# The short branch's output projection by seven half-block products in two duals, with its operands' sums behind the last input dual

## The chip, the cores and the metric

The kernel is written for one Trainium2 core and runs on one. Its time is device microseconds of one execution; the kernel before has a median of 1498.0 us over three runs (1496.49 to 1498.34). The engines are TensorE (PE, with its weight loads as PEld), VectorE (DVE), ScalarE (ACT), GpSimd (POOL) and SyncE (SP), which here issues most of the loads. Each engine, and each queue of DMA issues, works through its own list in order; they meet through semaphores.

## The reference

One block of a streaming encoder on 1024 positions (T) of 1024 channels (D), in float32:

```
h    = rms_norm(x, g) * (1 + sc1) + sh1              # sh1, sc1, g1, ... = silu(c) @ w_ada + b_ada
b_s, c_s, v_s, v_c, gl_c, gates = split(h @ w_in)
y_a  = (b_s * causal_dwconv3(c_s * v_s)) @ w_short_out
u    = causal_dwconv31(v_c * sigmoid(gl_c)) + bias
y_b  = silu(layer_norm(u)) @ w_conf_out
g_a, g_b = split(sigmoid(gates))
x    = x + g1 * ((g_a * y_a + g_b * y_b) @ w_o)
x    = x + g2 * swiglu_ffn(rms_norm(x) * (1 + sc2) + sh2)
out  = rms_norm(x, g_final)
```

## The kernel before, in words

**Products.** A float32 product is made of three matmuls: an operand is split into a rounded high part and the rest (`split`: a cast on ACT, a subtraction on DVE), a weight likewise into `wh` and `wl` (`split_w`: the cast on ACT, `wl = raw - wh` on DVE or POOL), and `mm3` issues high by high, low by high and high by low (L286, L287, L289). Matmuls are 128x128 by 128x512; T is handled in halves of 512.

**Duals.** The input projection runs, after a lead, in 12 duals (`win_dual`). A dual treats two output column blocks together and multiplies 2 by 2 blocks with seven half-block products in place of eight, in the order `PRODUCTS` ("1265734"). Each of the seven takes 24 matmuls and its own weight tile, partly a sum of blocks of the matrix (`dual_units`: "s1" is a21+a22, and so on; in the duals POOL makes the sums and the low parts). Its results are sums of the products, made as they come out: `c11`, `c22`, `c12` and `c21` do that on DVE and ACT. `PAIRS` says which columns a dual makes: gates ("g"), products of the short branch ("p", "q"), or the conv branch's input ("u"). The short branch leaves `q`, eight tiles of 128 x 1024, stored to DRAM by `q_store`.

**Beside the duals** DVE runs the eight long convs, tap by tap (L674), paced over `CONV_DUALS` duals by `issue_after`; POOL adds each conv to a total (`add_conv`) for the layer norm.

**Then ya**, the product with `w_short`: eight column blocks (`col_block`), each with one weight tile of 1024 columns and 48 matmuls, giving both halves; DVE multiplies each by the gate `ga`, loaded by POOL's queue, into `ma` (L765). In between come mean and variance (`ln_mean`, `ln_square`, `ln_rstd`) and eight `modulation`s (a product of the conditioning vector with a column block of `w_ada`, one long DVE instruction each). `q_load` brings q back from DRAM in the last dual and splits all of it there.

**Then yb** (`row_blocks` over `w_conf`, with `act_b` one block ahead and 16 modulations, in `next_b`), where `gb` is multiplied in and `join` adds `ma`; **then** `mix` with `w_o`, and the feed-forward part, again in duals.

**What sets the order.** The code is written in the order in which a tile scheduler takes it; tiles come from pools whose buffers wait for their last reader (raw weights have 3 + 2 buffers, `wh` and `wl` 3 each, gate tiles 6, PSUM 6 + 2 banks). Weights are fetched `AHEAD` (2) units before use, from `plan`. Where the code says `issue_after`, an instruction is held behind another.

Of the kernel before, what the change touches and what calls it, by code (L numbers as in the profile page):

```python
# [37 lines left out]
ALU = mybir.AluOpType  # L38
# [44 lines left out]

CONV_DUALS = 11.2
AT_READS = {"7": 4.5, "3": 5.5, "4": 6.5}
# [25 lines left out]
def block_kernel(ctx: ExitStack, tc: tile.TileContext, x0, xT, c, vecs, ada, w_first, w_plain, w_duals,  # L111
# [101 lines left out]

    def dual_units(mats, n, early=False, eng=nc.vector):

        a = {}

        def get(*blocks):
            for b in blocks:
                a[b] = load(mats[("11", "12", "21", "22").index(b)], n)  # L220

        def unit(m):
            if early:
                get(*{"1": ("11",), "2": ("12",), "6": ("21", "22", "11"), "3": ("12",), "4": ("22",)}.get(m, ()))
            elif m == "1":
                get("11", "12", "21", "22")
            if m in "12":
                return split_w(a["1" + m], n, (), eng)
            if m == "6":
                a["s1"] = a["22"] if early else raw_tile(n)  # L230
                eng.tensor_tensor(a["s1"], a["21"], a["22"], ALU.add)  # L231
# [4 lines left out]
            return split_w(a[{"6": "11", "5": "s1", "7": "21", "3": "12", "4": "22"}[m]], n, (), eng)  # L236

        return {m: (lambda m=m: unit(m)) for m in PRODUCTS}
# [314 lines left out]

    qT = [[None, None] for _ in range(KC)]

    def q_load(j):

        t = uc_tile("q", T)
        nc.sync.dma_start(t, q_dram[j])
        for h in range(2):  # L560
            qT[j][h] = split(t[:, halves[h]], hl_tile, f"q{j}{h}")

    def win_dual(d, pairs, x, y, z):
# [4 lines left out]
        def c11(p, e, kind, j, *more):  # L568
            if kind == "q":
                times(sc[j][:, halves[0]], y[p], sc[j][:, halves[0]])  # L570
                return
            if kind == "u":
                u.append(u_tile(j))
                e["b"] = [u[j][:, CK - 1 + h * H : CK - 1 + (h + 1) * H] for h in range(2)]
            elif kind == "p":
                e["t"] = uc_tile(f"p{j}", T + SK - 1)
                nc.vector.memset(e["t"][:, : SK - 1], 0.0)
                e["b"] = [e["t"][:, SK - 1 + h * H : SK - 1 + (h + 1) * H] for h in range(2)]
            else:
                e["t"] = [uc_tile("sig", T) for _ in range(2)]  # L580
                e["b"], e["c"] = ([t[:, s] for s in halves] for t in e["t"])
            nc.scalar.activation(e["b"][0], y[p], AF.Sigmoid if kind == "g" else AF.Copy)

        def c22(p, e, kind, j, *more):
            src = y[p] if kind == "q" else e["5"]
            add = nc.vector.tensor_tensor(src, x[p], e["5"], ALU.add)
            if kind == "q":
                return minus_times(sc[j + 1][:, halves[1]], src, sc[j + 1][:, halves[1]])
            if kind == "p":
                e["z"] = src  # L590
            else:
                e["z"] = e["c"][1] if kind == "g" else src
                nc.scalar.activation(e["z"], src, AF.Sigmoid, scale=-1.0)
            return add

        def c12(p, e, kind, j, *more):
# [5 lines left out]
            if kind == "p":  # L602
                return minus_times(e["b"][1], z[p], e["z"])
            nc.scalar.activation(e["b"][1], z[p], AF.Sigmoid)
            return add

        def c21(p, e, kind, j, *more):
# [7 lines left out]
            nc.scalar.activation(e["c"][0], x[p], AF.Sigmoid, scale=-1.0)  # L615

        banks = {"1": x, "6": x, "7": x, "4": x, "2": y, "5": z, "3": z}
        for m in PRODUCTS:
            w = next_w()
            for p in range(2):  # L620
# [9 lines left out]
                else:  # L630
                    done = {"2": c11, "7": c22, "3": c12, "4": c21}[m](p, e, *pairs[p])
                    if done is not None:
                        reads.append((7 * d + AT_READS[m] + 0.5 * p, done.ins))
            if d == len(PAIRS) // 2 - 1 and m in "1265":
                for j in range(2):
                    q_load(2 * "1265".index(m) + j)
        for e, (kind, j, *more) in zip(st, pairs):
            if kind == "p":
                short_conv(j, e["t"], x)
            elif kind == "q":  # L640
                for i in range(2):
                    q_store(j + i)
            elif kind == "g":
                for g, t in zip((j, *more), e["t"]):
                    nc.scalar.dma_start(gate_dram[g], t)

# [43 lines left out]
    def add_conv(j):  # L690

        with tc.issue_after(pool_los[min(int(7 * CONV_DUALS * (j + 1) / KC) + 5, len(pool_los) - 1)]):
            for h in range(2):
                nc.gpsimd.tensor_tensor(tot[h], tot[h], u[j][:, halves[h]], ALU.add)
# [6 lines left out]
    def ln_mean():  # L701
        mu = []
        for h in range(2):
            mps = ps_tile("mu")
# [19 lines left out]
    def ln_rstd(sqs):  # L724
        rs = []
        for h in range(2):
            var = ps_tile("var")
            nc.tensor.matmul(var, ones, sqs[h], start=True, stop=True)
# [10 lines left out]
    def act_b(k, h):  # L739
        z = cv[k][:, halves[h]]  # L740
        with ExitStack() as order:
            if (KC - 1, 1) in ma:
                order.enter_context(tc.issue_after(ma["ins"]))
# [15 lines left out]
    ma = {}  # L759
    for j in range(KC):  # L760
        for h, ps in enumerate(col_block(next_w(), qT, (0, 1), "ya")):
            ga = g_tile("ga")
            nc.gpsimd.dma_start(ga, gate_dram["a", j][:, halves[h]])
            ma[j, h] = s_tile(f"ma{j}{h}")
            ma["ins"] = nc.vector.tensor_tensor(ma[j, h], ps, ga, ALU.mult).ins  # L765
        if j == 0:
            mu = ln_mean()
        if j < 5:
            for i in range((0, 1, 3, 5, 7)[j], (1, 3, 5, 7, 8)[j]):
                ln_square(i)  # L770
        if j == 5:
            rl = ln_rstd(sqs)
        if j == KC - 2:
            act_b(0, 0)
        if j < KC - 2:
            modulation(16 + j)


    modulation(22)
    modulation(23)  # L780
    mg = [[None, None] for _ in range(KC)]
# [441 lines left out]
```

## Time and profile before

| | |
|---|---|
| three runs | 1496.49, 1498.34, 1498.0 us; median 1498.0 |
| profiled execution | 1498.83 us, of which the span is 1497.1 us |
| TensorE clock granted, mean | 0.996 |
| last input dual | 534.3 to 572.4 us, PE busy 38.10 of 38.10 |
| ya with mean and variance | 572.4 to 663.1 us, PE busy 90.70 of 90.70, DVE 54.89, POOL 26.53, DMA share 0.59 |
| yb | 663.1 to 754.4 us, PE busy 87.82 of 91.30, DVE 74.24, POOL 7.52, DMA share 0.60 |
| mix | 754.4 to 841.0 us, PE busy 86.60 of 86.60, DVE 57.74, POOL 16.76, DMA share 0.58 |

All times of the profile come from one execution. Busy time is time in which an engine had an instruction running. A stretch in which PE is busy throughout is one that only fewer matmuls can shorten. "`<-DVE gb`" in a wait names what came last of the things waited for.

### The profile page before, as it was taken

Reading aid. Unit: us, or ns where it says so; the run is one execution under the profiler, and the core shown is the slowest. Engines: PE = TensorE matmul, PEld = TensorE weight load, DVE = VectorE, ACT = ScalarE, POOL = GpSimd, SP = SyncE. Lnnn points to the kernel's source line nnn. Section 1 sums busy time; section 2 is a strip of 40 time slices with the busy share of each in tenths; the row PEclk is TensorE's granted clock in tenths of the full one; section 3 lists DMA queues with packets and bytes.
Section 4 is the critical chain, followed back from the end, with each engine's and each line's share of the span. In section 5 each row is a group of like instructions: output and inputs, shape, how many; then the busy total and the mean of one; then the engine's idle time right before and its main releaser. Section 6 shows DMA issues by size and latency. Waiting matters only on the chain.

```text
span 1497.1 us, 17720 instructions
## 1 busy us (share of the span) xinstructions
PE 1467.0 (98%) x6455; PEld 1201.2 (80%) x6455; DVE 1140.8 (76%) x1569; ACT 623.8 (42%) x896; POOL 537.7 (36%) x467
## 2 busy tenths in 40 slices
PE   6999999999999999999999999999999999999997
PEld 2788888888888788888788878888888888888887
DVE  7994999887887984767767699977666665677755
ACT  4653434343443353245335464544444443222235
POOL 0037777777767773410121001110000016545005
PEclk9999999999999999999999999999999999999999
DMA  9512223232222268455765437654444449998403
GB/s 352 208 65 70 99 71 113 70 99 85 99 71 85 99 248 314 148 185 167 245 203 165 140 113 267 231 167 150 149 148 154 151 151 356 362 313 263 134 28 113
DMA packets 83129, 248.82 MB, mean 166 GB/s; under 512 B 9569, under 2 KB 11745, under 8 KB 83042
## 3 DMA queue, kind: packets, MB, share of 16 engines
q1 hardware_dynamic: 42208, 139.48, 27.9%
q0 software_dynamic: 36944, 95.44, 19.4%
q10 hardware_dynamic: 3890, 12.78, 2.2%
q8 instruction: 50, 0.82, 0.2%
q14 instruction: 37, 0.30, 0.1%
HBM read 185.27 MB, written 62.39 MB: 165 GB/s over the span
## 4 chain that ended last, share of the span: by engine, by line
PE 91%; DVE 5%; issue 1%; DMA 1%; ACT 1%; POOL 0%; POOLq 0%; ACTq 0%; DVEq 0%
PE x L286 10%; PE x L289 10%; PE x L287 10%; PE z L286 7%; PE z L287 7%; PE z L289 7%; PE y L286 6%; PE y L289 6%; PE y L287 6%; PE ya L289 2%; PE ya L286 2%; PE ya L287 2%; PE mix L286 2%; PE mix L287 2%; PE mix L289 2%; PE yb L289 2%
## 5 line engine op out<-in xcount | busy, mean ns | idle before, releaser
L208 ACT CAST wh<-raw 128x1024 fp32r<-128x1024 f32 (+2 forms) x257 | 259.3, 1010 | 484.0 <-PE x L287 124.4
L209 POOL TENSOR_TENSOR wl<-raw,wh 128x1024 fp32r<-128x1024 f32 x92 | 227.5, 2474 | 131.0 <-ACT wh L208 127.2
L209 DVE TENSOR_TENSOR wl<-raw,wh 128x1024 fp32r<-128x1024 f32 (+2 forms) x165 | 188.2, 1141 | 65.2 <-ACT wh L208 62.4
L674 DVE SCALAR_TENSOR_TENSOR c<-diff,vec,c 128x512 f32<-128x512 f32 x248 | 178.6, 751 | 3.3
L942 POOL DMA_DIRECT2D hid<-stage x71 | 37.7, 532 | 354.2 <-DVE stage L326 353.5
L286 PE MATMUL x<-th,wh 128*128 128x512 f32 x240 | 93.4, 389 | 0.0
L289 PE MATMUL x<-th,wl 128*128 128x512 f32 x240 | 93.4, 389 | 0.0
L287 PE MATMUL x<-tl,wh 128*128 128x512 f32 x240 | 93.4, 389 | 0.0
L674 DVE SCALAR_TENSOR_TENSOR c<-u,wsum,c 128x512 f32<-128x512 f32 x112 | 84.1, 751 | 1.8
L267 DVE CUSTOM_DVE_ANT_0 raw<-raw,cs,vec 128x1024 f32<-128x1024 f32 x24 | 35.4, 1481 | 51.2 <-DMA raw<-in_ada 51.2
L286 PE MATMUL z<-th,wh 128*128 128x512 f32 x168 | 65.4, 389 | 0.0
L287 PE MATMUL z<-tl,wh 128*128 128x512 f32 x168 | 65.4, 389 | 0.0
L289 PE MATMUL z<-th,wl 128*128 128x512 f32 x168 | 65.4, 389 | 0.0
L231 POOL TENSOR_TENSOR raw<-raw 128x1024 f32<-128x1024 f32 x12 | 29.8, 2483 | 95.1 <-DVE wl L209 94.3
L325 ACT CAST stage<-g 128x512 fp32r<-128x512 f32 x62 | 38.3, 621 | 53.6 <-DMA hid<-stage 27.4
L326 DVE TENSOR_TENSOR stage<-g,stage 128x512 fp32r<-128x512 f32 x62 | 42.4, 687 | 20.8 <-ACT stage L325 20.7
L968 POOL DMA_DIRECT2D th<-hid x71 | 38.0, 535 | 50.9 <-PE x L289 28.5
L286 PE MATMUL yb<-zsh,wh 128*128 128x512 f32 x128 | 50.0, 391 | 3.5 <-DVE gb L796 3.5
L286 PEld LDWEIGHTS x<-th,wh 128*128 128x128 f32 x240 | 45.1, 188 | 9.5 <-issue 0.2
L289 PEld LDWEIGHTS x<-th,wl 128*128 128x128 f32 x240 | 45.1, 188 | 9.4
L287 PEld LDWEIGHTS x<-tl,wh 128*128 128x128 f32 x240 | 45.0, 188 | 9.3
L286 PE MATMUL y<-th,wh 128*128 128x512 f32 x132 | 51.3, 389 | 0.0
(1012 smaller groups left out, 4256.7 us busy)
## 6 DMA issues: line engine op xcount, KB each, us to landing
hid<-stage POOLq DMA_DIRECT2D x71, 512.0 KB, 4.5
raw<-in_w_fi SPq DMA_DIRECT2D x53, 512.0 KB, 4.2
raw<-in_w_duals SPq DMA_DIRECT2D x48, 512.0 KB, 3.5
th<-hid POOLq DMA_DIRECT2D x71, 256.0 KB, 5.7
tl<-hid POOLq DMA_DIRECT2D x71, 256.0 KB, 5.7
ada<-in_ada SPq DMA_DIRECT2D x24, 512.0 KB, 6.1
raw<-in_ada SPq DMA_DIRECT2D x24, 512.0 KB, 4.6
raw<-in_w_fo SPq DMA_DIRECT2D x24, 384.0 KB, 5.9
```

What stands on the lines that cost most here:

```text
L208: nc.scalar.copy(wh, raw)
L209: lo = lo_engine.tensor_tensor(wl, raw, f32(wh), ALU.subtract)
L231: eng.tensor_tensor(a["s1"], a["21"], a["22"], ALU.add)
L267: nc.vector.tensor_tensor_reduce(out=raw, in0=raw, in1=cs, scale=1.0, scalar=col(V_ADA, b), op0=ALU.mult, op1=ALU.add, accum_out=modc(b),)
L286: nc.tensor.matmul(ps, wh, xh, start=first, stop=False, skip_group_check=again)
L287: nc.tensor.matmul(ps, wh, xl, start=False, stop=False, skip_group_check=again)
L289: mm3.ins = nc.tensor.matmul(ps, wl, xh, start=False, stop=last, skip_group_check=again).ins
L325: nc.scalar.copy(hi, src)
L326: t_split.ins = nc.vector.tensor_tensor(lo, src, f32(hi), ALU.subtract).ins
L674: tap.ins = nc.vector.scalar_tensor_tensor(out=out, in0=src[:, s : s + H], scalar=wt, in1=acc, op0=ALU.mult, op1=ALU.add).ins
L942: nc.gpsimd.dma_start(hid_dram[key], s)
L968: nc.gpsimd.dma_start(t, hid_dram[key][:, s])
```

## The change

1. The product with `w_short` runs as two duals of seven half-block products (`ya_product`; order `ya_order`): products 1 and 2 of both duals first, then 65734 of each. The matmuls are 2 x 7 x 24 in place of 8 x 48.
2. Its weights are units of `dual_units`, 16 loads of 512 KB in place of 8. POOL makes the four sums of each dual and the low parts of 1 and 2, DVE the low parts of the other five.
3. q's operands: the eight q tiles are combined in place (`q_operands`: 16 subtractions, 28 splits on ACT and DVE, in place of 16 splits), each product's set in the last dual or ya, behind the sums that make that dual's results. q4 to q7 stay in their tiles; only q0 to q3 are stored and loaded again.
4. Gates are written to DRAM by halves (`gate_out`); the gate loads of ya go through SP's queue into the `ma` tiles themselves.
5. Nine modulations move from ya and yb into the first nine duals; eight stay in yb's first half, seven go to mix's first half. The convs are paced over 10.8 duals (11.2), and `add_conv` waits for two units in place of five.
6. Mean and variance use the other PSUM pool, and ya's first product is held behind the last dual's last matmul, which keeps TensorE's order.

```diff
-CONV_DUALS = 11.2
+CONV_DUALS = 10.8
+MOD_DUALS = 9
...
-    plan += [(w_short[k], 1024, (), nc.gpsimd) for k in range(KC)]
+    ya_order = [(d, m) for d in range(2) for m in "12"] + [(d, m) for d in range(2) for m in PRODUCTS[2:]]
+    ya_units = [dual_units([w_short[d, m] for m in range(4)], 1024, True, nc.gpsimd, {m: nc.vector for m in "65734"})
+                for d in range(2)]
+    plan += [ya_units[d][m] for d, m in ya_order]
...
+    def gate_out(g, h, src, t, scale=1.0):
+
+        nc.scalar.activation(t, src, AF.Sigmoid, scale=scale)
+        nc.scalar.dma_start(gate_dram[g][:, halves[h]], t)
...
-        t = uc_tile("q", T)
-        nc.sync.dma_start(t, q_dram[j])
-        for h in range(2):
-            qT[j][h] = split(t[:, halves[h]], hl_tile, f"q{j}{h}")
+        sc[j] = uc_tile("q", T)
+        nc.sync.dma_start(sc[j], q_dram[j])
...
+    def q_operands(m):
+
+        for k in range(KH):
+            b11, b12, b21, b22 = (q_block(k, i) for i in range(4))
+            if m == "6":
+                nc.vector.tensor_tensor(b11, b11, b12, ALU.subtract)
+                t2 = g_tile("t2")
+                minus(t2, b11, b22)
+                tq[m][k] = split(t2, hl_tile, "tq")
+                minus(b21, t2, b21)
+                continue
+            if m == "7":
+                nc.vector.tensor_tensor(b12, b22, b12, ALU.subtract)
+            tq[m][k] = split({"1": b11, "2": b21, "5": b11, "7": b12, "3": b22, "4": b21}[m], hl_tile, "tq")
...
-            if d == len(PAIRS) // 2 - 1 and m in "1265":
-                for j in range(2):
-                    q_load(2 * "1265".index(m) + j)
+            if m == "2" and d < MOD_DUALS:
+                modulation(16 + d, uc_tile("ada", D))
+            if d == len(PAIRS) // 2 - 1:
+                if m == "1":
+                    for j in range(KH):
+                        q_load(j)
+                if m in "16734":
+                    q_operands({"1": "1", "6": "2", "7": "6", "3": "5", "4": "7"}[m])
...
-        modulation(24 + KC * h + k)
+        if h == 0:
+            modulation(16 + MOD_DUALS + k)
...
-        for h, ps in enumerate(col_block(next_w(), qT, (0, 1), "ya")):
-            ga = g_tile("ga")
-            nc.gpsimd.dma_start(ga, gate_dram["a", j][:, halves[h]])
-            ma[j, h] = s_tile(f"ma{j}{h}")
-            ma["ins"] = nc.vector.tensor_tensor(ma[j, h], ps, ga, ALU.mult).ins
...
+        if m in "2734":
+            for p in range(2):
+                j, h = 2 * (2 * d + p) + (m in "74"), int(m in "73")
+                ma[j, h] = ga[p] = s_tile(f"ma{j}{h}")
+                nc.sync.dma_start(ga[p], gate_dram["a", j][:, halves[h]])
+        for p in range(2):
+            ps = bank[p]
+            for k in range(KH):
+                c0 = (p * KH + k) * P
+                mm3([ps], slice(c0, c0 + P), w, [tq[m][k]], m in "15" and k == 0, k == KH - 1, m not in "15")
+            if m == "1":
+                nc.scalar.copy(ya_banks[d]["y"][p], ps)
+            elif m in "65":
+                ya_rest[p, m] = s_tile("v")
+                nc.scalar.copy(ya_rest[p, m], ps)
+            elif m == "2":
+                ma["ins"] = times(ga[p], ps, ga[p]).ins
...
+    for i, (d, m) in enumerate(ya_order):
+        with ExitStack() as order:
+            if i == 0:
+                order.enter_context(tc.issue_after(mm3.ins))
+            ya_product(d, m)
+        if i in (0, 3):
+            q_operands("34"[i == 3])
+        elif i == 2:
             mu = ln_mean()
...
+            if h == 0 and j < KC - 1:
+                modulation(16 + MOD_DUALS + KC + j)
```

POOL at the turn from the last dual to ya; `wl` is a weight's low part, `raw` on the left a sum of weight blocks, `ga` a gate load. Before (the first two `wl` rows here belong to the last dual, the other four to `w_short`):

```order
L209 TENSOR_TENSOR wl_3803<-raw_3567,wh_3802 128x1024 [waits PE_49,Activation_49]
L763 DMA ga_4468<-gate_a0_107 128x512 [waits DVE_49]
L209 TENSOR_TENSOR wl_3855<-raw_3571,wh_3854 128x1024 [waits PE_49,Activation_49]
L694 TENSOR_TENSOR tot0_975<-tot0_975,u7_2980 128x512
L694 TENSOR_TENSOR tot1_976<-tot1_976,u7_2980 128x512
L763 DMA ga_4472<-gate_a0_107 128x512 [waits DVE_49]
L209 TENSOR_TENSOR wl_3889<-raw_3886,wh_3888 128x1024 [waits DMAHW6_49,PE_49,Activation_49]
L209 TENSOR_TENSOR wl_3923<-raw_3920,wh_3922 128x1024 [waits DMAHW0_49,PE_49,Activation_49]
L209 TENSOR_TENSOR wl_4415<-raw_4412,wh_4414 128x1024 [waits DMAHW1_49,PE_49,Activation_49]
L209 TENSOR_TENSOR wl_4496<-raw_4493,wh_4495 128x1024 [waits DMAHW2_49,PE_49,Activation_49]
```

After the change (the first row is the last dual's; the next `wl` are of dual 0's products 1 and 2, then dual 1's):

```order
L210 TENSOR_TENSOR wl_3844<-raw_3603,wh_3843 128x1024 [waits PE_49,Activation_49]
L210 TENSOR_TENSOR wl_3912<-raw_3909,wh_3911 128x1024 [waits DMAHW1_49,PE_49,Activation_49]
L233 TENSOR_TENSOR raw_4559<-raw_4557,raw_4559 128x1024 [waits DMAHW7_49,DMAHW1_49,Pool_49]
L210 TENSOR_TENSOR wl_3964<-raw_3961,wh_3963 128x1024 [waits DMAHW5_49,PE_49,Activation_49]
L234 TENSOR_TENSOR raw_4557<-raw_4557,raw_4561 128x1024 [waits DMAHW6_49,Pool_49]
L210 TENSOR_TENSOR wl_4476<-raw_4473,wh_4475 128x1024 [waits PE_49,Activation_49]
L235 TENSOR_TENSOR raw_4561<-raw_4561,raw_4559 128x1024 [waits Pool_49]
L210 TENSOR_TENSOR wl_4524<-raw_4521,wh_4523 128x1024 [waits DMAHW2_49,PE_49,Activation_49]
L237 TENSOR_TENSOR raw_4684<-raw_4684,raw_4561 128x1024 [waits DMAHW3_49,Pool_49]
```

Between the low parts now stand the sums of dual 0's blocks; the `tot` sums and the gate loads are no longer among them.

SP at the same place; `raw<-in_w_short` is a weight load, `cv` the reload of a conv, `ma<-gate_a` a gate load. Before:

```order
L194 DMA raw_4412<-in_w_short 128x1024 [waits DMAHW1_49,Pool_49]
L194 DMA raw_4493<-in_w_short 128x1024
L194 DMA raw_4577<-in_ada 128x1024 [waits DMAHW3_49,Pool_49]
L714 DMA cv0_4482<-cv0_967 128x1024 [waits DMAHW5_49,DMAHW4_49,DVE_49]
L714 DMA cv1_4557<-cv1_968 128x1024 [waits DMAHW6_49,DVE_49]
L714 DMA cv2_4567<-cv2_969 128x1024 [waits Pool_49]
L714 DMA cv3_4644<-cv3_970 128x1024 [waits DMAHW7_49,DMAHW0_49,DVE_49]
L194 DMA raw_4667<-in_w_short 128x1024 [waits DMAHW1_49,Pool_49]
```

After the change:

```order
L195 DMA raw_4559<-in_w_short 128x1024 [waits DMAHW1_49,Pool_49]
L195 DMA raw_4561<-in_w_short 128x1024 [waits DMAHW6_49,DMAHW5_49,Pool_49]
L741 DMA cv0_4719<-cv0_967 128x1024 [waits DMAHW7_49,DVE_49]
L741 DMA cv1_4727<-cv1_968 128x1024 [waits DMAHW1_49,DVE_49]
L741 DMA cv2_4775<-cv2_969 128x1024 [waits DMAHW2_49,DVE_49]
L195 DMA raw_4684<-in_w_short 128x1024 [waits DMAHW3_49,Pool_49]
L195 DMA raw_4737<-in_w_short 128x1024 [waits DMAHW4_49,Pool_49]
L801 DMA ma00_4527<-gate_a0_107 128x512 [waits DMAHW5_49,PE_49]
L801 DMA ma20_4529<-gate_a2_109 128x512 [waits DMAHW6_49,DMAHW0_49,PE_49]
L801 DMA ma40_4606<-gate_a4_111 128x512 [waits DMAHW7_49,PE_49]
L801 DMA ma60_4608<-gate_a6_113 128x512 [waits DMAHW0_49,PE_49]
L741 DMA cv3_4785<-cv3_970 128x1024 [waits DMAHW1_49,DVE_49]
```

The gate loads of product 2 of both duals now stand on SP, behind the two weight loads; each of those waits for a step of POOL, the second for the low part of (dual 1, product 2).

DVE where yb's first results come; `gb` is a gate times a result, `cv` the layer norm's scaling, ISA a modulation. Before:

```order
L209 TENSOR_TENSOR wl<-raw,wh 128x1024 x2
L267 ISA raw,mod<-raw,cs,vec 128x1024
L267 ISA mod 128x1
L796 TENSOR_TENSOR gb<-yb_5054,gb 128x512
L796 TENSOR_TENSOR gb<-yb_5055,gb 128x512
L796 TENSOR_TENSOR gb<-yb_5056,gb 128x512
L784 TENSOR_TENSOR gb<-gb,ma_4470 128x512
```

After the change:

```order
L210 TENSOR_TENSOR wl<-raw,wh 128x1024
L771 TENSOR_TENSOR cv_4936<-cv_4936,rl1r 128x512
L278 SCALAR_TENSOR_TENSOR aff_105<-mod,vec 128x1
L210 TENSOR_TENSOR wl<-raw,wh 128x1024
L857 TENSOR_TENSOR gb<-yb_5115,gb 128x512
L857 TENSOR_TENSOR gb<-yb_5116,gb 128x512
L845 TENSOR_TENSOR gb<-gb,ma_4527 128x512
L845 TENSOR_TENSOR gb<-gb,ma_4864 128x512
```

The modulation ahead of the first `gb` is gone.

More of the change, by code (lines that the diff above doesn't have):

```diff
@@ L579, in c11 @@
             else:
-                e["t"] = [uc_tile("sig", T) for _ in range(2)]
-                e["b"], e["c"] = ([t[:, s] for s in halves] for t in e["t"])
-            nc.scalar.activation(e["b"][0], y[p], AF.Sigmoid if kind == "g" else AF.Copy)
+                return gate_out(j, 0, y[p], g_tile("sig"))
+            nc.scalar.copy(e["b"][0], y[p])
         def c22(p, e, kind, j, *more):
@@ L588, in c22 @@
                 return minus_times(sc[j + 1][:, halves[1]], src, sc[j + 1][:, halves[1]])
[L589 to L593, printed above, removed]
+            e["z"] = src
+            if kind == "g":
+                gate_out(more[0], 1, src, src, -1.0)
+            elif kind == "u":
+                nc.scalar.activation(src, src, AF.Sigmoid, scale=-1.0)
             return add
@@ L614, in c21 @@
                 return times(e["b"][0], x[p], e["b"][0])
[L615 removed]
+            gate_out(more[0], 0, x[p], g_tile("sig"), -1.0)
         banks = {"1": x, "6": x, "7": x, "4": x, "2": y, "5": z, "3": z}
@@ L639, in win_dual @@
                 short_conv(j, e["t"], x)
-            elif kind == "q":
+            elif kind == "q" and j < KH:
                 for i in range(2):
                     q_store(j + i)
-            elif kind == "g":
-                for g, t in zip((j, *more), e["t"]):
-                    nc.scalar.dma_start(gate_dram[g], t)
     taps = vec[:, V_CW : V_CW + CK // 2 * 2 * KC].rearrange("p (j two k) -> p j two k", two=2, k=KC)
@@ L767, in block_kernel @@
+    for i, (d, m) in enumerate(ya_order):
[6 more added lines that the diff above has]
+        elif i == 2:
             mu = ln_mean()
[L768 to L771, printed above, removed]
+        elif 5 <= i < 10:
+            for j in range(*((0, 2), (2, 4), (4, 6), (6, 7), (7, 8))[i - 5]):
+                ln_square(j)
+        elif i == 10:
```

47 lines of the change are left out of this document (30 added, 17 removed).

## The prediction

> **What bounds the kernel now.** I read the page's busy times and chain first, then what TensorE waits for.
>
> ```profile
> span 1497.1 us, 17720 instructions
> PE 1467.0 (98%) x6455; PEld 1201.2 (80%) x6455; DVE 1140.8 (76%) x1569; ACT 623.8 (42%) x896; POOL 537.7 (36%) x467
> PE 91%; DVE 5%; issue 1%; DMA 1%; ACT 1%; POOL 0%; POOLq 0%; ACTq 0%; DVEq 0%
> ```
>
> TensorE is busy for 98% of the span and makes 91% of the chain that ended last. The profiled execution took 1498.83 us, 1.7 us more than this span, and the three timed runs have a median of 1498.0; so I sum against the profiled execution and put the sum on 1498.0.
>
> The waits of TensorE, longest first:
>
> ```profile
> PE ss L407 <- DVE sq L401: 6.1, 1, 6.1
> PE lead L282 <- ACT x L357: 4.6, 1, 4.6
> PE yb L286 <- DVE gb L796: 3.5, 2, 1.8
> PE z L286 <- ACT g L917: 3.2, 1, 3.2
> ```
>
> Only the third lies near the change. The others are in the lead and the feed-forward part, which the change leaves alone. In the stretches that the change touches, the columns being PE, PEld, DVE, ACT and POOL busy, clock, DMA share and GB/s:
>
> ```profile
> 530.00:572.00 42.00, 42.00 (x187) 34.75 (x186) 32.99 (x38) 24.11 (x39) 27.55 (x14) 1.00 0.79 293
> 572.00:600.00 28.00, 28.00 (x121) 22.50 (x120) 11.71 (x18) 7.74 (x12) 7.18 (x6) 1.00 0.79 300
> 600.00:630.00 30.00, 30.00 (x134) 24.83 (x133) 25.15 (x33) 9.79 (x14) 13.62 (x11) 1.00 0.46 143
> 700.00:754.00 54.00, 50.52 (x222) 41.19 (x221) 45.73 (x75) 18.05 (x25) 5.38 (x10) 1.00 0.64 211
> 170.00:210.00 40.00, 39.20 (x173) 32.15 (x172) 38.64 (x54) 15.63 (x22) 30.43 (x14) 1.00 0.20 66
> 210.00:250.00 40.00, 40.00 (x179) 33.10 (x178) 38.42 (x58) 15.14 (x21) 28.89 (x14) 1.00 0.35 122
> ```
>
> The last dual (530 to 572) and ya (from 572) run with TensorE never idle and at full clock. So each matmul taken out of ya is worth its whole pitch, as long as nothing new keeps TensorE waiting. VectorE (DVE) is nearly full in the early duals, and the DMA engines carry 0.79 around the start of ya.
>
> **Part 1, 48 matmuls less.** The chain gives the pitch: in ya, six matmuls pass between two lines of the same kind.
>
> ```profile
> 572.81 0.23 PE ya L287
> 573.04 0.23 PE ya L286
> 573.49 0.45 PE ya L289 x2
> 574.17 0.23 PE ya L287
> ```
>
> 574.17 − 572.81 = 1.36 us for six, 0.2267 us each. The product has 8 × 48 = 384 of them now, and 2 × 7 half-block products of 24 = 336 then: 48 × 0.2267 = 10.9 us less. The mean and variance matmuls stay. One half-block product takes 24 × 0.2267 = 5.44 us.
>
> **Part 2, the stall in yb.** The first wait for gb is VectorE being late: its sum over `yb` stands behind a modulation that waited for its weights. The second is a gate load.
>
> ```profile
> 700.15 1.28 DVE L267 CUSTOM_DVE_ANT_0 raw<-raw,cs,vec 128x1024 f32<-128x1024 f32 x1 [2.25 <-DMA raw<-in_ada]
> 701.37 1.88 DVE L796 TENSOR_TENSOR gb<-yb,gb 128x512 f32<-128x512 f32 x3
> 716.94 0.69 DVE L796 TENSOR_TENSOR gb<-yb,gb 128x512 f32<-128x512 f32 x1 [1.81 <-DMA gb<-gate_b]
> ```
>
> In the new order no modulation stands ahead of the first `gb`, and none is left in yb's second half. The gate load of the second wait is issued once an `mg` split has freed a buffer, and those splits come earlier with the first. I take −3.0 of the 3.5 us; it can't be more than −3.5, and 0 if the second half still waits for something. What would be late next there is the rescaled weights' low part, which VectorE then makes ahead of `gb`.
>
> **Part 3, the front of ya.** This is the chain I expect to cost most. The weight sums are made on GpSimd (POOL) between the low parts, their raw buffers are refilled by SP, and SP's queue holds the new gate loads behind two weight loads. The rows for it:
>
> ```profile
> L209 POOL TENSOR_TENSOR wl<-raw,wh 128x1024 fp32r<-128x1024 f32 x92 | 227.5, 2474 | 131.0 <-ACT wh L208 127.2
> L231 POOL TENSOR_TENSOR raw<-raw 128x1024 f32<-128x1024 f32 x12 | 29.8, 2483 | 95.1 <-DVE wl L209 94.3
> 566.39 3.50 POOL L209 TENSOR_TENSOR wl<-raw,wh 128x1024 fp32r<-128x1024 f32 x1 [2.42 <-ACT wh L208]
> raw<-in_w_short SPq DMA_DIRECT2D x8, 512.0 KB, 5.2
> ga<-gate_a POOLq DMA_DIRECT2D x16, 256.0 KB, 3.2
> L765 DVE TENSOR_TENSOR ma<-ya,ga x16: 673/680/691, 588.8 to 663.6; 128x512 f32<-128x512 f32 x16
> 569.28 0.60 ACT L604 ACTIVATE sig<-y 128x512 f32<-128x512 f32 x1 [0.40 <-ACT sig L604]
> ```
>
> A POOL step is 2.4 to 2.5 us, a weight load lands 5.2 us after issue, a gate load 3.2 us after. Write (d,m) for product m of ya's dual d; the order is (0,1), (0,2), (1,1), mean, (1,2), then the rest. TensorE wants (0,1) at 572.4, (0,2) at 577.8, (1,1) at 583.2, and (1,2) at 590.4 (two products of 5.44 and the mean's 1.7 later). POOL's first low part for w_short now starts at 566.39 and takes 3.5. The new one has the same buffer to wait for, but no `tot` sums just ahead of it; I put its end at about 566.8. The step after it needs a block whose buffer that low part frees: load landed 572.0, first sum to 574.4, low part of (0,2) to 576.8, in time by 1 us. Again a load (582.0), sum (584.4), low part of (1,1) (586.8). TensorE wants that from its third matmul, at 583.6: 3.2 us late. Then the sum to 589.2 and the low part of (1,2) to 591.6.
>
> The gate loads of (0,2) are queued on SP behind the weight load that waits for that last low part. So they land at 591.6 + 3.2 = 594.8; two multiplies of 0.68 and one copy of 0.60 must pass before (1,2) may write the same banks: 596.7 against 590.4, 6.3 us late in all. With the first low part 2 us sooner it is 4.3. I take +5.5. The lower bound is +1.5 (half of the DMA trips hidden behind products that have slack), the upper +9 (landings of 6 to 7 us, as the q loads show below, on DMA engines at 0.79).
>
> ```profile
> q<-q SPq DMA_DIRECT2D x8, 512.0 KB, 6.8
> ```
>
> Queued behind the waiting gate loads on SP is a load of a conv (`cv`) and the next weight loads; the mean and `rl` that need them have products of five groups to hide under.
>
> **Part 4, q's operands.** Sums and splits: 28 splits and 16 subtractions of 128x512 in the last dual and ya, where 16 splits were. 28 more by 0.60 us (pitch, below) is 17 us of VectorE; it has 42.0 − 33.0 = 9.0 us free in 530 to 572 and 16.3 in 572 to 600, and the modulations that stood there are gone. So they fit, in sum. But some run into POOL:
>
> ```profile
> 551.52 0.68 DVE L318 TENSOR_TENSOR q21l<-q,q21h 128x512 fp32r<-128x512 f32 x1
> 552.90 2.49 DVE L318 TENSOR_TENSOR q30l<-q,q30h 128x512 fp32r<-128x512 f32 x1 [0.70 <-ACT q30h L317]
> 555.31 0.68 DVE L318 TENSOR_TENSOR q31l<-q,q31h 128x512 fp32r<-128x512 f32 x1
> 552.43 2.41 POOL L209 TENSOR_TENSOR wl<-raw,wh 128x1024 fp32r<-128x1024 f32 x1 [3.64 <-ACT wh L208]
> 600.75 3.69 DVE L716 TENSOR_TENSOR cv<-cv,tot 128x512 f32<-128x512 f32 x6
> 601.68 5.03 POOL L209 TENSOR_TENSOR wl<-raw,wh 128x1024 fp32r<-128x1024 f32 x1
> ```
>
> The same split takes 0.68 alone, and 2.49 when a POOL step began 0.5 us before it; the other way round, a POOL step issued into a run of VectorE sums took 5.03 instead of 2.41, 2.6 longer. The Trainium skill (SBUF — State Buffer, Who interferes with whom) says that a VectorE instruction with two inputs in SBUF and a GpSimd instruction that reads SBUF exclude one another for a whole instruction; these rows agree, and the rule speaks against this change, which brings more such VectorE work beside more such POOL steps. From the rows alone: the operands have the slack of a product each, so VectorE's own delay is hidden; POOL's isn't, and is in the upper end of part 3. In ya's second half six more VectorE streams (conv subtractions, squares, low parts, `ma`) meet the four POOL sums of the last products: I take +1.5, from 0 to +5 (two such collisions of 2.6).
>
> **Part 5, the duals.** Nine modulations of 1.28 us move there from ya and yb, and the convs are paced over 10.8 duals instead of 11.2. The taps:
>
> ```profile
> L674 DVE SCALAR_TENSOR_TENSOR c<-diff,vec,c 128x512 f32<-128x512 f32 x248 | 178.6, 751 | 3.3
> L674 DVE SCALAR_TENSOR_TENSOR c<-u,wsum,c 128x512 f32<-128x512 f32 x112 | 84.1, 751 | 1.8
> ```
>
> They are 262.7 us, 23.5 in each of 11.2 duals or 24.3 in each of 10.8. VectorE has 40.0 − 38.5 = 1.5 us free in 40 in the early duals. One modulation a dual and the faster taps ask for 1.3 + 0.8, so it runs about 0.6 us behind each dual, for four duals or so, until the load falls. TensorE waits only when an evacuation is later than the slack of about one product. I take +1.0, from 0 to +3. Gates written by halves, the q blocks kept on chip (half of the stores and loads go) and 16 weight loads in place of 8 about balance on the DMA engines; I take 0, hidden beside TensorE.
>
> **The sum.** −10.9 − 3.0 + 5.5 + 1.5 + 1.0 = −5.9: the profile would show 1492.9, and the runs 1492.1 us.
>
> **The rivals.**
>
> *The full gain.* POOL starts its low parts earlier than I think, since `tot` is out of the way, and the weight loads land in 3.5 us as those of the duals do. Then ya has at most a microsecond of waits and the time is 1498.0 − 10.9 − 3.0 + 1.0 = 1485.1. For it: TensorE never waits in ya now. Against: two loads wait in turn for low parts in POOL's order, and nothing shortens those trips.
>
> *No difference.* Part 3 comes to its upper end, 9, part 4's to 3.5 and the wait in yb stays in its second half (−1.7): −10.9 − 1.7 + 9 + 3.5 + 1 = +0.9, but with one of them milder −2 to −3: 1496.
>
> *Slower, by one mechanism: POOL locked out by VectorE.* The place is POOL's eight steps from 566 to 592, which alternate with a backlog of about 30 back-to-back operand sums and splits. Each collision of the size of 601.68 costs 2.6 us on the chain of part 3. With five of them, 13 us come on top of the 5.5: −10.9 − 3.0 + 5.5 + 13 = +4.6, and 1502.6. It decides from 13.9 us of waits in ya on: about three such collisions more than my central case has. For it speaks that VectorE's operands have all their inputs and so issue without gaps; against, that four of the eight steps begin after a DMA trip of 5 us, in which VectorE can work off its backlog.
>
> *The change doesn't do what it says* would need TensorE's products to wait for q's operands themselves; the first set comes after the last dual's first product, with over 30 us to go. I give it nothing of its own.
>
> **How the numbers follow.** My case, waits in ya and the duals of 4 to 11 us with the result 1488 to 1495, has 0.5; the full gain 0.13, no difference 0.17, slower 0.2. About 0.2%, 3 us, is what the runs can tell from no change. Faster by more: my case and the full gain, 0.63; within 0.2%: 0.17; slower: 0.2. The range reaches from the full gain, 1485.1 less part 5's microsecond (1484), to the slower rival with its collisions, 1502.6, rounded to 1503. My case's own range is 1488 to 1495.
>
> **What would show it.** TensorE's matmul count falls by 48, to about 6407; the waits have no `yb <- gb` of more than 1 us. In ya the waits of TensorE should be of product (1,1) for a low part made by POOL, and of (1,2) for an ACT copy that follows a gate load, together 4 to 7 us, with POOL steps of 2.4 and gaps of about 5 between them. Wrong I would be if ya's waits are under 1.5 us or above 11, if VectorE's evacuations of the early duals show waits over 3 us in sum, or if the operands of q are what TensorE waits for.

## The result, and the profile after

The changed kernel takes 1492.9 us (median of ten runs, 1491.71 to 1495.84) against 1498.3 for the kernel before beside it: a ratio of 0.9969, with a 95% interval of 0.9961 to 0.9977. That is 5.4 us less; forecast were 5.9 less. Its profiled execution took 1494.31 us.

The first lines of the changed kernel's page, and TensorE's waits between 560 and 660 us (engine, line, what was waited for: sum, times, longest):

```profile
span 1492.5 us, 17732 instructions
PE 1458.9 (98%) x6407; PEld 1192.0 (80%) x6407; DVE 1186.0 (79%) x1615; ACT 643.6 (43%) x926; POOL 554.4 (37%) x455
```

```profile
PE z L294 <- POOL wl L210: 3.0, 1, 3.0
PE y L291 <- ACT y L808: 1.7, 1, 1.7
PE x L291 <- DVE v L816: 1.3, 1, 1.3
PE x L291 <- DVE ma L554: 0.7, 1, 0.7
PE z L294 <- DVE wl L210: 0.5, 1, 0.5
PE y L294 <- POOL wl L210: 0.4, 1, 0.4
```

The 48 matmuls are gone (6455 to 6407), `yb <- gb` is in no wait any more, and ya, which had none, waits six times. The two stretches, ya and yb, by the same columns as before:

```profile
571.10:662.20 91.10, 83.53 (x346) 65.15 (x346) 73.32 (x89) 44.08 (x66) 38.97 (x15) 0.98 0.58 201
662.20:749.60 87.40, 87.32 (x386) 72.00 (x385) 68.94 (x101) 41.96 (x57) 6.44 (x12) 1.00 0.55 179
```

So ya is as long as it was, with 336 products' matmuls in place of 384, and yb is 3.7 us shorter. This table gives the length of the stretches, in us, from the first matmul of each to the first of the next in the profile (for all kernels told of below too; the ratio is to the kernel before as it ran beside each, with its 95% interval). "Lead" is the time up to the first `gb` product, which differs by over 1 us among profiles of kernels that are the same there.

| kernel | us | ratio | lead | duals | ya | yb |
|---|---|---|---|---|---|---|
| before | 1498.3 | | 102.0 | 470.4 | 90.6 | 91.1 |
| changed | 1492.9 | 0.9969 (0.9961 to 0.9977) | 102.5 | 468.6 | 91.0 | 87.4 |
| before, 48 matmuls less | 1492.5 | 0.9959 (0.9945 to 0.9973) | 102.9 | 470.4 | 79.7 | 95.0 |
| changed, gate loads on ACT | 1492.0 | 0.9960 (0.9947 to 0.9973) | 103.1 | 468.7 | 89.1 | 87.5 |
| changed, low parts on DVE | 1490.1 | 0.9944 (0.9931 to 0.9957) | 102.5 | 468.7 | 87.9 | 87.4 |
| changed, mean before (1,1) | 1495.2 | 0.9977 (0.9968 to 0.9985) | 103.1 | 468.7 | 92.1 | 87.4 |
| changed, dual 1's sums on DVE | 1491.0 | 0.9946 (0.9933 to 0.9959) | 102.6 | 468.6 | 88.0 | 88.2 |
| changed, all sums on DVE | 1488.6 | 0.9929 (0.9915 to 0.9943) | 102.8 | 468.7 | 84.9 | 89.4 |
| changed, 16 modulations in yb | 1494.6 | 0.9974 (0.9962 to 0.9987) | 101.8 | 468.6 | 91.0 | 87.5 |
| changed, convs and totals as before | 1507.1 | 1.0050 (1.0037 to 1.0063) | 102.3 | 472.9 | 98.2 | 89.0 |
| changed, convs as before | 1504.4 | 1.0033 (1.0021 to 1.0046) | 102.0 | 473.2 | 97.7 | 87.4 |
| before, ya's modulations in duals | 1493.9 | 0.9971 (0.9958 to 0.9983) | 101.8 | 469.7 | 90.6 | 87.0 |
| before, new pace of convs | 1496.3 | 0.9988 (0.9980 to 0.9997) | 101.8 | 469.0 | 90.6 | 91.0 |
| changed, two shifts to DVE, later splits | 1484.3 | 0.9906 (0.9893 to 0.9920) | 102.5 | 468.6 | 80.8 | 88.9 |

By the profiles, then: duals −1.8, ya +0.5 (−10.9 for the matmuls, +11.4 for gaps and slow matmuls), yb −3.7, lead +0.5, the rest +0.3, in sum −4.2 up to the last matmul. The two profiled executions lie 4.5 us apart (1498.83 and 1494.31), the medians 5.4.

The front of ya ran as the prediction had worked it out, step by step and within 1.3 us at each. POOL, whose rows these are, then a gate load's evacuation on DVE, the copy on ACT and the first matmul of (1,2):

```profile
563.33 4.81 POOL L210 TENSOR_TENSOR wl<-raw,wh 128x1024 fp32r<-128x1024 f32 x1 [4.62 <-ACT wh L209]
572.43 2.41 POOL L233 TENSOR_TENSOR raw<-raw 128x1024 f32<-128x1024 f32 x1 [4.29 <-issue]
574.79 2.86 POOL L210 TENSOR_TENSOR wl<-raw,wh 128x1024 fp32r<-128x1024 f32 x1
581.63 2.42 POOL L234 TENSOR_TENSOR raw<-raw 128x1024 f32<-128x1024 f32 x1 [3.99 <-DMA raw<-in_w_short]
584.01 2.33 POOL L210 TENSOR_TENSOR wl<-raw,wh 128x1024 fp32r<-128x1024 f32 x1
588.64 2.39 POOL L210 TENSOR_TENSOR wl<-raw,wh 128x1024 fp32r<-128x1024 f32 x1
```

```profile
595.31 1.41 DVE L557 TENSOR_TENSOR ma<-y,ma 128x512 f32<-128x512 f32 x2 [3.20 <-DMA ma<-gate_a]
596.09 0.57 ACT L808 COPY y<-z 128x512 f32<-128x512 f32 x1 [5.81 <-DVE ma L557]
596.72 0.50 PE L291 MATMUL y<-tqh,wh 128*128 128x512 f32 x1 [1.68 <-ACT y L808]
```

The low parts of (0,1), (0,2), (1,1) and (1,2) ended at 568.1, 577.7, 586.3 and 591.0 (forecast 566.8, 576.8, 586.8, 591.6), and (1,2) began at 596.72 (forecast 596.7). That this last step agrees to the digit is luck: the steps before it are off by −0.6 to +1.3 us, the gates were there 0.5 us later than forecast, and the copy began before the second multiply had ended.

### The profile page after: what moved, and what is told of

It is laid out like the page before. It is cut to its first block, busy times and chain, and to the rows that moved or that the text cites. A ratio compares the mean times of both kernels' runs of the same rounds, so it can differ in the third digit from the quotient of the medians.

```text
span 1492.5 us, 17732 instructions
## 1 busy us (share of the span) xinstructions
PE 1458.9 (98%) x6407; PEld 1192.0 (80%) x6407; DVE 1186.0 (79%) x1615; ACT 643.6 (43%) x926; POOL 554.4 (37%) x455
## 4 chain that ended last, share of the span: by engine, by line
PE 39%; issue 15%; POOL 3%; DVE 3%; DMA 2%; ACT 0%; POOLq 0%; DVEq 0%; ACTq 0%; SPq 0%
PE x L291 7%; PE x L292 7%; PE x L294 7%; PE z L292 3%; PE z L291 3%; PE z L294 3%; PE y L294 2%; PE y L292 2%; PE y L291 2%; DMA hid<-stage 1%; DVE cv L743 1%; DMA raw<-in_w_short 1%; PE yb L292 1%; PE yb L294 1%; PE yb L291 1%
## 5 line engine op out<-in xcount | busy, mean ns | idle before, releaser
L209 ACT CAST wh<-raw 128x1024 fp32r<-128x1024 f32 (+2 forms) x263 | 265.6, 1011 | 454.0 <-PE z L292 129.3
L210 DVE TENSOR_TENSOR wl<-raw,wh 128x1024 fp32r<-128x1024 f32 (+2 forms) x175 | 201.3, 1151 | 83.6 <-ACT wh L209 81.5
L210 POOL TENSOR_TENSOR wl<-raw,wh 128x1024 fp32r<-128x1024 f32 x88 | 219.9, 2502 | 108.4 <-ACT wh L209 108.4
L233 POOL TENSOR_TENSOR raw<-raw 128x1024 f32<-128x1024 f32 x14 | 42.7, 3053 | 116.9 <-DVE wl L210 94.9
L272 DVE CUSTOM_DVE_ANT_0 ada<-ada,cs,vec 128x1024 f32<-128x1024 f32 x33 | 48.5, 1486 | 7.9 <-DMA ada<-in_ada 7.9
L292 PE MATMUL y<-tl,wh 128*128 128x512 f32 x132 | 51.3, 389 | 0.0
```

The source lines that it names most:

```text
L209: nc.scalar.copy(wh, raw)
L210: lo = lo_engine.tensor_tensor(wl, raw, f32(wh), ALU.subtract)
L272: nc.vector.tensor_tensor_reduce(out=raw, in0=raw, in1=cs, scale=1.0, scalar=col(V_ADA, b), op0=ALU.mult, op1=ALU.add, accum_out=modc(b),)
L292: nc.tensor.matmul(ps, wh, xl, start=False, stop=False, skip_group_check=again)
```

## The experiments

**What the matmuls are worth.** In the kernel before, with the eighth row block skipped, so that this block's part is missing from its result:

```diff
-        for k in range(KC):
-            mm3(outs, slice(k * P, k * P + P), w, [act[k][h] for h in hs], k == 0, k == KC - 1)
+        n = KC - 1 if name == "ya" else KC
+        for k in range(n):
+            mm3(outs, slice(k * P, k * P + P), w, [act[k][h] for h in hs], k == 0, k == n - 1)
```

> The kernel before, with the last of the eight row blocks of the product with w_short left out (48 matmuls less; this part of y_a is missing from the result) and nothing else changed. If each matmul of ya is worth its pitch of 0.2267 us, ya is 10.9 us shorter in the profile (79.8 us instead of 90.7) and the time falls by 10.9 us, to about 1487. If something else than TensorE paced ya (loads at a DMA share of 0.8, gates, q's splits), it falls by less, and the new wait shows in ya.

ya became 10.9 us shorter, to 79.7, just the pitch. But the time fell by 5.9 only: yb became 95.0 us long. Its waits:

```profile
PE yb L286 <- DVE gb L797: 3.9, 1, 3.9
PE yb L286 <- DVE ma L766: 0.8, 1, 0.8
PE yb L287 <- DVE zsl L319: 0.3, 1, 0.3
```

The sum over `yb` stands behind a modulation that waits for its weights, as in the kernel before, and longer (4.36 us instead of 2.25):

```profile
694.06 1.28 DVE L267 CUSTOM_DVE_ANT_0 raw<-raw,cs,vec 128x1024 f32<-128x1024 f32 x1 [4.36 <-DMA raw<-in_ada]
```

A shorter ya brings yb's products up before what they need is made; 3.9 us, a third of the gain, was given back there.

**Which wait ends last at (1,2).** First the gate loads of product 2, on ACT's queue:

```diff
-                nc.sync.dma_start(ga[p], gate_dram["a", j][:, halves[h]])
+                (nc.scalar if m == "2" else nc.sync).dma_start(ga[p], gate_dram["a", j][:, halves[h]])
```

> The changed kernel, with the four gate loads of product 2 of both duals issued from ACT's queue instead of SP's, so that they stand behind no weight load. If the gate loads are what product (1,2) waits for, they land before 588 and (1,2) starts where the mean ends, near 594.9 instead of 596.7: 1.9 us less, 1491 us. If the low part of (1,2), the evacuation of (0,2) on DVE or the bank is what ends last, (1,2) starts at 596 to 597 as now, and the time is the same.

The wait of (1,2) for the copy is gone from the list, and ya is 1.9 us shorter, though (1,1) waited 3.8 us here instead of 3.0. The gate loads were what (1,2) waited for. The time itself, 1492.0, can't be told from the 1492.9 of the changed kernel (the intervals overlap). Then the mean one product earlier (`elif i == 1: mu = ln_mean()` in place of `i == 2`):

> The changed kernel, with the four matmuls of the mean (1.7 us) ahead of product (1,1) instead of behind it. If the waits simply add up, the mean fills 1.7 us of the 3.0 us wait of (1,1): 1.7 us less, and less of the slow stretch behind the wait, 1489 to 1491. If (1,2)'s start is set by the chain POOL, weight load, gate load, whatever TensorE does before, it still starts at about 596.7: the wait moves from (1,1) to (1,2), and the time is the same within 1 us, or longer by up to 2 us if a wait of over 3 us is followed by slow matmuls.

The start of (1,2), with its wait:

```profile
597.52 0.80 PE L291 MATMUL y<-tqh,wh 128*128 128x512 f32 x1 [5.22 <-ACT y L808]
```

Work put into the first wait came back as a longer second: (1,2) began at 597.5 (596.7 in the changed kernel, whose ya began 0.6 earlier), and ya is 1.1 us longer. The chain by the weight loads and the gate loads sets this start, whatever TensorE does ahead of it.

**POOL's chain.** The low parts of dual 1's products 1 and 2 on DVE:

```diff
-    ya_units = [dual_units([w_short[d, m] for m in range(4)], 1024, True, nc.gpsimd, {m: nc.vector for m in "65734"})
-                for d in range(2)]
+    ya_units = [dual_units([w_short[d, m] for m in range(4)], 1024, True, nc.gpsimd,
+                           {m: nc.vector for m in ("65734", "6573412")[d]}) for d in range(2)]
```

> The changed kernel, with the low parts of ya's second dual, products 1 and 2, made by DVE instead of POOL. POOL then makes only sums between 577 and 592. If POOL's alternation of low parts, sums and DMA trips makes the two waits at the front of ya (3.1 us with 1.9 us of slow matmuls behind it, and 1.9 us), both go, since the weight loads ahead of the gate loads are released earlier too: 5 to 7 us less, 1486 to 1488. If POOL is late because DVE locks it out, DVE's two added low parts do not change that, and the waits turn up at DVE or at the sums: 0 to 2 us less.

ya is 3.1 us shorter, less than by the first theory and more than by the second. The wait at (1,1) is gone, but (1,2) now waits 3.0 us for the same copy. DVE and POOL there:

```profile
582.71 8.46 DVE L323 TENSOR_TENSOR tql<-sc,tqh 128x512 fp32r<-128x512 f32 x3
592.23 1.28 DVE L557 TENSOR_TENSOR ma<-y,ma 128x512 f32<-128x512 f32 x2
```

```profile
585.12 2.73 POOL L235 TENSOR_TENSOR raw<-raw 128x1024 f32<-128x1024 f32 x1
587.93 2.70 POOL L237 TENSOR_TENSOR raw<-raw 128x1024 f32<-128x1024 f32 x1
```

Three splits that take 0.68 each took 8.46 while POOL's sums followed one another, and the evacuation that frees the bank stands behind them on DVE. So both theories hold a part: POOL's chain makes the first wait; with it gone, DVE, held up beside POOL's sums, makes the next.

**The second half.** In the changed kernel, POOL and DVE from 611 on:

```profile
611.20 10.54 POOL L233 TENSOR_TENSOR raw<-raw 128x1024 f32<-128x1024 f32 x1 [16.87 <-DVE sq L749]
621.82 2.73 POOL L234 TENSOR_TENSOR raw<-raw 128x1024 f32<-128x1024 f32 x1
```

```profile
620.02 2.28 DVE L743 TENSOR_TENSOR cv<-cv,tot 128x512 f32<-128x512 f32 x1
622.22 2.88 DVE L554 SCALAR_TENSOR_TENSOR ma<-v,ma 128x512 f32<-128x512 f32 x1
625.03 2.88 DVE L743 TENSOR_TENSOR cv<-cv,tot 128x512 f32<-128x512 f32 x1
```

First a run of DVE work holds one POOL sum for 10.5 us; from then on single DVE operations take 2.3 to 2.9 us beside the sums. With dual 1's sums on DVE (`(nc.gpsimd, nc.vector)[d]` for the engine of the sums, the low parts of 1 and 2 left on POOL):

> The changed kernel, with the four weight sums of ya's second dual made by DVE (about 1.2 us each) instead of POOL. In the changed kernel one of these sums took 10.5 us on POOL from 611 on, and single DVE operations beside them 2.3 to 2.9 us instead of 0.7. If the two engines locking each other out makes the second half's waits (1.5, 0.6 and 0.9 us of gaps between 626 and 639), no DVE operation there takes over 1.3 us, two or all three of the gaps go, and ya is 2 to 3 us shorter. If DVE is late because it has too much to do, 4.8 us more work on it makes the waits longer by up to 4.8.

The changed kernel's three gaps between 626 and 639 (1.5, 0.6 and 0.9 us between matmuls beyond their pitch; in the list of waits they are the 1.3, 0.5 and 0.7) are all gone, ya is 3.0 us shorter, and DVE shows such rows as these, though it has more to do:

```profile
619.04 0.68 DVE L749 TENSOR_TENSOR sq<-sq 128x512 f32<-128x512 f32 x1
620.24 0.68 DVE L743 TENSOR_TENSOR cv<-cv,tot 128x512 f32<-128x512 f32 x1
620.84 0.68 DVE L554 SCALAR_TENSOR_TENSOR ma<-v,ma 128x512 f32<-128x512 f32 x1
```

The rule of the Trainium skill that the prediction weighed (SBUF — State Buffer, Who interferes with whom) is borne out here in both directions: 10.5 us for a sum of 2.4, 2.9 for an operation of 0.68.

**All the sums on DVE**, POOL keeping the four low parts of products 1 and 2, gate loads of product 2 on ACT:

> The changed kernel, with all eight weight sums of ya on DVE (POOL keeps only the four low parts of products 1 and 2) and the first four gate loads on ACT's queue. If DVE and POOL locking each other out, with SP's order, makes all of ya's waits, front and second half, ya is near its 336 matmuls and the mean and variance: 76.2 + 3.4 = 79.6 us instead of 91.0, so 1482 to 1484 with at most 2 us of waits left. If the weight loads' trips (raw buffers that are refilled late) make the front's waits, they stay at 3 us or more, and the time is 1486 to 1489.

ya is 84.9 us long, not 79.6, and the time of 1488.6 is the second theory's, as is a wait of over 3 us at the front. The second half has no wait left, but one of 3.5 us came up at (0,2): DVE's first sum waits for its blocks (a load, and the buffer that POOL's low part frees), and the last dual's sum `y` stands behind it.

```profile
572.60 1.23 DVE L233 TENSOR_TENSOR raw<-raw 128x1024 f32<-128x1024 f32 x1 [2.90 <-POOL wl L210]
573.74 0.69 DVE L622 TENSOR_TENSOR y<-y,v 128x512 f32<-128x512 f32 x1
```

A wait that POOL could afford is not one that DVE can.

**Why yb's wait went.** Sixteen modulations back in yb (eight in the duals, none in mix):

> The changed kernel, with sixteen modulations in yb as before (eight of them in its second half), eight in the duals, none in mix. If the modulations in front of gb make the wait in yb, the wait comes back: yb is 91 us as in the kernel before (or 95, as with 48 matmuls less and the modulations left in yb) instead of 87.4, so 1496 to 1500. If yb is shorter for another reason (the gate tiles, the order of gate loads), it stays near 87.4 and the time near 1493.

yb is 87.5: the modulations of its second half are not the cause. Then the other side, the kernel before with only ya's eight moved into the duals (`if m == "2" and d < KC: modulation(16 + d, uc_tile("ada", D))`, and none in ya):

> The kernel before, with only the eight modulations of ya moved, into the first eight duals; the sixteen in yb stay. If the wait of yb came from modulation loads that were late because ya's eight stood ahead of them, it goes: yb is near 87.5 us instead of 91.1. If the modulations in yb's own second half make it, it stays near 91. The eight modulations in the duals should cost there what they cost in the changed kernel with the old pace of the convs (472.9 against 470.4 us): 2 to 2.5 us. So 1496 to 1498 by the first, 1499 to 1501 by the second.

yb is 87.0 us, with TensorE never idle in it:

```profile
662.10:749.10 87.00, 87.00 (x385) 72.09 (x384) 73.93 (x115) 41.08 (x57) 7.52 (x14) 1.00 0.62 201
```

So it was ya's modulations. One in yb still stands ahead of the first `gb` and still waits for its weights, but 33.2 us after yb's start instead of 37.2, and `gb` is in time:

```profile
695.27 1.29 DVE L267 CUSTOM_DVE_ANT_0 raw<-raw,cs,vec 128x1024 f32<-128x1024 f32 x1 [3.68 <-DMA raw<-in_ada]
697.61 1.28 DVE L792 TENSOR_TENSOR gb<-yb,gb 128x512 f32<-128x512 f32 x2
```

This edit by itself makes the kernel before about 4.5 us faster (0.9971), nearly as much as the whole change. The forecast of 2 to 2.5 us of cost in the duals was wrong; they became 0.7 us shorter. Why, no run shows.

**The pace of the convs.** In the changed kernel `CONV_DUALS` back to 11.2 and the totals to five units:

> The changed kernel, with the convs paced over 11.2 duals and the totals five units behind, as before. If the pace of the convs took the two waits of the duals away (1.0 us at 194 and 1.1 at 500 to 504 before the change), they come back and the duals are 464.5 us instead of 462.7; the time is 1 to 2 us longer. If the gates by halves or the moved modulations did it, the duals stay at 462.7. If convs that end later make ya's front later (its q operands and cv loads stand behind them), ya is longer than 91.0 by 1 to 3 us.

The ratio goes from 0.9969 to 1.0050, 12 us, far more than any theory said: slower than the kernel before. With the pace alone put back:

> The changed kernel, with only the convs paced over 11.2 duals again; the totals stay two units behind. If the taps that run on into the last dual are what cost 13 us (they ended at 525 in the changed kernel and at 551 with the old pace and the old totals), the last taps end at about 550 and the time is 1504 to 1508. If it was the totals on POOL, five units behind, the time stays within 3 us of 1493.

1504.4 and a ratio of 1.0033: most of it is the pace, about 10 us. SP issued q3's reload at this time in the changed kernel:

```profile
532.60 0.33 SPq L567 DMA_DIRECT2D q<-q  x1
```

The rows of the run with the old pace for SP, ACT and DVE:

```profile
557.82 0.33 SPq L567 DMA_DIRECT2D q<-q  x1
```

```profile
561.24 0.62 ACT L322 CAST tqh<-q 128x512 fp32r<-128x512 f32 x1 [4.27 <-DMA q<-q]
```

```profile
549.53 1.53 DVE L701 SCALAR_TENSOR_TENSOR c<-diff,vec,c 128x512 f32<-128x512 f32 x2
561.89 0.69 DVE L323 TENSOR_TENSOR tql<-q,tqh 128x512 fp32r<-128x512 f32 x1 [10.82 <-ACT tqh L322]
```

The last taps ran to 551 instead of 525, q3's reload, whose tile reuses a buffer of the convs, was issued 25 us later, and DVE stood still for 10.8 us in front of a split, with the last dual's results and the other operands behind it. SP's wait for that reload names what it stood behind, the store of a conv, which is issued once the taps are done. In ya TensorE then waits longest for the cast of a weight on ACT, which came after those late results and casts:

```profile
SPq L567 <- DMA cv<-u: 5.4, 1, 5.4
```

```profile
587.02 0.79 PE L291 MATMUL z<-tqh,wh 128*128 128x512 f32 x1 [6.21 <-ACT wh L209]
```

That the pace costs the 10 us is shown; that the shared buffer is the way is read from these rows, since no run gave q3's tile a buffer of its own. In the kernel before the same pace is worth little:

> The kernel before, with only the convs paced over 10.8 duals and the totals two units behind. If the pace is what takes waits out of the duals, they are 468.6 to 469.5 us instead of 470.4 (the waits at 194 and 500 to 504 go), and the time falls by 1 to 2 us. If the pace only pays together with q's operands in the last dual (as the 13 us that it was worth in the changed kernel suggest), the duals stay at 470 or more, and the time is the same or longer.

The duals are 1.5 us shorter: the waits at 500 to 504 went, the one at 194 stayed.

**A faster version.** Dual 1's low parts and sums on DVE, dual 0's sums left on POOL, and the splits for products 3 and 4 later (`if i in (3, 4): q_operands("34"[i == 4])`):

> The changed kernel, with the low parts of ya's second dual and that dual's sums on DVE (the changes of two runs together; the first dual's sums stay on POOL), and the operand sets of products 3 and 4 of q split one to two products later, so that the evacuation of (0,2) does not stand behind splits that POOL locks out. If the locks are what is left, the wait of 3.1 us for that evacuation goes too: ya 83 to 85 us, 1485 to 1487. If the gate loads or the weight loads end just as late, ya is 85 to 86 (the gains of the two runs added, 3.1 + 3.0) and the time 1487 to 1488.

1484.3 us, a ratio of 0.9906 (0.9893 to 0.9920), some 9 us less than the change. ya is 80.8 us with TensorE busy for nearly all of it, and its only wait there is 0.2 us:

```profile
571.10:651.90 80.80, 80.43 (x346) 64.35 (x344) 72.69 (x95) 43.85 (x66) 15.77 (x9) 1.00 0.64 220
```

```profile
PE yb L291 <- DVE ma L554: 0.5, 1, 0.5
PE yb L292 <- DVE zsl L323: 0.3, 1, 0.3
PE var L755 <- DVE sq L749: 0.2, 1, 0.2
```

These are all the waits that it has between 560 and 760 us. It was better than the expectation, by which ya would be 83 to 86 us long. What the later splits bring by themselves was not tried.

## Why the prediction was right, and where it wasn't

The time was forecast within 1 us, but four terms of the sum were off and cancelled: parts 3 and 4 cost 4.4 us more than forecast, parts 2 and 5 together 3.5 less. That the total came so near is luck. In ya the gaps took all that the 48 matmuls gave; what is left of the gain lies in yb and the duals.

*Part 1, −10.9*: shown, by leaving 48 matmuls out. That it adds up with the others was assumed: by itself it would have brought 7.0 in ya and yb together.

*Part 2, −3.0*: measured −3.7, a little past the bound of −3.5. The step that gave it is not the reason: "no modulation stands ahead of the first `gb`, and none is left in yb's second half" held here, but yb is as short, 87.0, in the kernel before with ya's eight moved, where both still stand there. The reason is that ya's modulations are gone. And since a shorter ya alone made yb 95.0, moving them is worth some 7.6 us beside part 1 (95.0 against 87.4, from two kernels that differ in more than this).

*Part 3, +5.5*: the chain came out step by step, and both waits were named. The size failed at its last step: the prediction worked out 6.3 and took 5.5. Measured are 7.6: (1,2) was due 18.0 us after ya's start at 571.15 and began at 596.72. The 1.3 us between lie in the duals: they ended earlier, while POOL and the loads did not. (The waits listed for the whole of ya also sum to 7.6; that is chance.)

*Part 4, +1.5*: measured 3.8 (the 11.4 us of gaps less the 7.6). The two engines holding each other up was weighed, with more of it than the 2.6 us of the row it was priced by (one sum took 8.1 us longer). But the step that VectorE's own delay is hidden failed: the three gaps are waits for results of DVE, whose operations took 2.3 to 2.9 us beside POOL's sums.

*Part 5, +1.0*: measured −1.8. The step that failed prices modulations and pace by DVE's load alone; in the kernel before, eight modulations made the duals 0.7 us shorter and the pace 1.5. And the sum had no term for what the faster pace saves in the changed kernel, where the taps must end before the last dual, for q's reload needs their buffer: about 10 us hang on it. A slower result was there to be had with the old pace, and not by the rival's way of POOL locked out. (Ahead of the result 16 weight loads were counted; the changed kernel's page has 14, and no term rests on the difference.)

By the prediction's own mark, waits in ya above 11 would make it wrong. The listed waits sum to 7.6, but with the short gaps and slow matmuls around them ya lost 11.4; the terms for ya were too small, and the duals and yb paid for it.

## What to carry to other kernels

Removing matmuls from a stage that TensorE fills was worth their pitch there (10.9 us), and then the stage after it must be read anew: its operands have that much less time. Where a buffer chain runs through two queues that keep their order (POOL's sums, SP's loads), its end could here be worked out from rows to within 1.3 us, and work moved into a wait ahead of that end bought nothing. Before an edit is priced by its own work, ask which buffer it frees and when: a number that looked like pacing held up a reload.

## What the runs showed of the hardware that was not expected

In the changed kernel a wait of TensorE of about 3 us is followed by slow matmuls, one of 1.7 us is not. Clock and matmuls behind the waits of (1,1) and (1,2) in the changed kernel (the clock is the last column but two):

```profile
586.40:590.20 3.80, 3.80 (x10) 2.99 (x11) 0.41 (x1) 1.49 (x2) 3.80 (x2) 0.55 0.42 138
596.70:600.70 4.00, 3.98 (x16) 3.02 (x17) 3.91 (x7) 3.98 (x7) 0.00 (x0) 1.00 1.01 395
```

Behind the first, of 2.97 us, matmuls came every 0.43 us instead of 0.23 for 3.8 us at a granted clock of 0.55: 1.9 us more. (They cost nothing there, as the gate loads set the start of (1,2).) In the run with the mean first the wait of 5.2 us was followed by the same, at 0.50:

```profile
597.50:601.30 3.80, 3.78 (x9) 3.02 (x10) 3.80 (x7) 3.05 (x5) 0.00 (x0) 0.50 1.03 408
```

The length of the wait does not decide alone. With the old pace put back, a wait of 1.82 us was followed by slow matmuls too, at 0.55; with the old totals beside it, one of 1.81 us at the same place (638.80) was followed by a clock of 1.00. The first of the two, and the clock behind it:

```profile
636.74 0.68 PE L291 MATMUL x<-tqh,wh 128*128 128x512 f32 x1 [1.82 <-DVE v L816]
636.70:640.50 3.80, 3.76 (x10) 2.94 (x11) 3.80 (x6) 3.03 (x4) 0.00 (x0) 0.55 0.39 135
```

The Trainium skill (TensorE: Matmul & The Clock Gate, Part 1: The HAM clock gate) puts the slow state behind an idle window of about 3.4 us, and says that this window runs free of the kernel; here waits of 3.0 and once of 1.8 us were enough, and what tells the two of 1.8 us apart no run shows.
